# Issuing the second input load ahead of SyncE's arrival at the entry barrier

## Chip, cores, metric

One core of one Trainium2 chip; the other cores of the chip run nothing of this program. The metric is the device time of one execution in microseconds, the median of several runs.

## The reference

Each row of a 1024 x 4096 float32 matrix is divided by its length:

```python
def reference(x, axis, eps):            # axis = -1, eps = 1e-12
    norm = np.sqrt(np.sum(x ** 2, axis=axis, keepdims=True) + eps)
    return (x / norm).astype(np.float32)
```

16.78 MB are read and 16.78 MB written. There is little arithmetic.

## The kernel before

The rows are cut into two groups. A group is one tile of 128 partitions x 4 rows x 4096 elements, 64 KB a partition, moved by one load and one store of 8.39 MB each. Both loads are issued by SyncE before any work; the stores are issued by SyncE as well, each when its group is done. ScalarE squares and sums three rows of a group and VectorE one; VectorE does most of the scaling.

The program begins with a barrier at which all engines meet. The kernel before already moves its first load to the front of it, when the program is finalized:

```python
def first_load_to_front(nc, load):
    def move(program):
        blocks = program.main_func.blocks
        entry = blocks[0].instructions
        ...                                   # body: the block that holds the load; at: its place
        assert not body[at].sync_info.on_wait
        before = next(n for n, i in enumerate(entry)
                      if i.engine == SP and isinstance(i, InstDrain))
        entry.insert(before, body.pop(at))    # ahead of SyncE's drain, its arrival at the barrier
    nc.at_finalize(move)

...
    for i in range(n_tiles):                  # n_tiles = 2
        g = RowGroups(nc, io, stats, scratch, D, R, eps_t)
        load = nc.sync.dma_start(out=g.flat(), in_=x_t[i])
        if i == 0:
            first_load_to_front(nc, load.ins)
        groups.append(g)

    for i, g in enumerate(groups):
        ...                                   # squares, norms, scalings of one group
        store = nc.sync.dma_start(out=out_t[i], in_=g.flat())
```

## Time and profile before

| | before |
|---|---|
| time, median of the first 3 runs | 81.92 us (81.86 to 81.96) |
| profiled execution: time, span | 82.04 us, 80.20 us |
| first load: issued, landed | 0.00, 22.06 us |
| second load: issued, landed | 0.79, 41.37 us |
| first store: issued, landed | 38.99, 60.72 us |
| second store: issued, landed | 56.76, 80.03 us |

"Issued" is the start of the issue on SyncE; "landed" is the last of the sixteen increments of the transfer's semaphore, one from each DMA engine. All are counted from the span's start. The four landings lie 19.31 to 19.35 us apart, whatever the four issue times are. The lines of the profile that carry this are in the prediction below.

### The profile page before, as it was taken

The numbers are of one execution on the slowest core, as the hardware profiler recorded it, in microseconds if no ns is written. First come the engines' busy times: TensorE is split into PE (matmuls) and PEld (weight loads), VectorE is DVE, ScalarE is ACT, GpSimd is POOL, SyncE is SP. The second block draws the span as 40 slices with busy tenths as digits, with TensorE's granted clock in tenths as the row PEclk, the third lists the DMA queues.
The fourth block names the chain that finished last, engine by engine and source line by source line (L and its number), as shares of the span: only waits on it lengthen the run. The fifth ranks groups of instructions, "written<-read, shape, count | busy, mean of one in ns | idle before, by whom it ended". The sixth has DMA issues, their size and how long they took to land.

```text
span 80.2 us, 93 instructions
## 1 busy us (share of the span) xinstructions
DVE 26.7 (33%) x21; ACT 29.7 (37%) x23; POOL 0.2 (0%) x4
## 2 busy tenths in 40 slices
DVE  0000000000099599960039995999200000000000
ACT  6000000000099999989439999950000000000000
POOL 0000000000000000000000000000000000000000
DMA  9099996699996699996699990999991999992990
GB/s 490 33 523 523 523 490 294 261 523 523 523 490 261 294 523 523 523 490 261 294 523 523 523 490 33 523 523 523 523 458 65 523 523 523 523 425 98 523 523 0
DMA packets 576, 33.55 MB, mean 418 GB/s; under 512 B 64, under 2 KB 64, under 8 KB 64
## 3 DMA queue, kind: packets, MB, share of 16 engines
q1 hardware_dynamic: 576, 33.55, 97.4%
HBM read 16.78 MB, written 16.78 MB: 418 GB/s over the span
## 4 chain that ended last, share of the span: by engine, by line
DMA 51%; ACT 10%; DVE 9%; issue 0%
DMA xt<-in_x_dram 51%; ACT sq_act L33 9%; DVE xt L64 9%; ACT rstd L53 1%; DVE rstd L59 0%
## 5 line engine op out<-in xcount | busy, mean ns | idle before, releaser
L33 ACT ACTIVATE sq_act<-xt 128x4096 f32<-128x4096 f32 x6 | 21.7, 3609 | 22.4 <-DMA xt<-in_x_dram 22.4
L42 DVE SCALAR_TENSOR_TENSOR sq_dve<-xt 128x4096 f32<-128x4096 f32 x2 | 8.9, 4426 | 26.4 <-DMA xt<-in_x_dram 26.4
L64 DVE TENSOR_SCALAR xt<-xt,rstd 128x4096 f32<-128x4096 f32 x7 | 16.5, 2353 | 0.2
L72 ACT ACTIVATE xt<-xt,rstd 128x3584 f32<-128x3584 f32 x1 | 3.3, 3283 | 0.2 <-DVE rstd L59 0.2
L53 ACT ACTIVATE rstd<-ssq,eps_t 128x1 f32<-128x1 f32 x8 | 2.1, 290 | 0.1
L59 DVE RECIPROCAL rstd<-rstd 128x1 f32<-128x1 f32 x8 | 1.3, 160 | 2.5 <-ACT rstd L53 2.5
L33 ACT ACT_TABLE_LOAD x1 | 1.3, 1283 | 0.8 <-PEq L258 0.8
L53 ACT ACT_TABLE_LOAD x1 | 1.3, 1283 | 0.0
L33 ACT ACTIVATION_READ_ACCUMULATOR sq_act<-xt 128x1 f32 x6 | 1.1, 187 | 0.0
L78 DVE TENSOR_SCALAR xt<-xt,rstd 128x512 f32<-128x512 f32 x1 | 0.5, 487 | 0.0
L211 DVE MEMSET eps_t<- 128x1 f32 x1 | 0.1, 59 | 0.9 <-PEq L258 0.9
L42 DVE DVE_READ_ACCUMULATOR sq_dve<-xt 128x1 f32 x2 | 0.2, 83 | 0.0
L258 POOL MEMSET const-uint8-127<- 128x1 uint8 x1 | 0.1, 103 | 0.0
L258 POOL MEMSET const-bfloat16-1.0<- 128x1 bf16 x1 | 0.1, 102 | 0.0
L258 POOL MEMSET const-float32-0.0<- 128x1 f32 x1 | 0.1, 99 | 0.2 <-issue 0.2
L258 POOL MEMSET const-float32-1.0<- 128x1 f32 x1 | 0.1, 99 | 0.0
## 6 DMA issues: line engine op xcount, KB each, us to landing
xt<-in_x_dram SPq DMA_DIRECT2D x2, 31.3
out_dram<-xt SPq DMA_DIRECT2D x2, 22.5
```

Of the source, the lines that this page charges most:

```text
L33: self.nc.scalar.activation(out=sq_a, in_=self.x[:, r], func=ACT_F.Square, accum_out=self.ssq[:, r : r + 1],)
L42: self.nc.vector.scalar_tensor_tensor(out=sq_v, in0=self.x[:, r], scalar=1.0, in1=self.x[:, r], op0=ALU.mult, op1=ALU.mult, accum_out=self ...
L53: self.nc.scalar.activation(out=self.rstd[:, r : r + n], in_=self.ssq[:, r : r + n], func=ACT_F.Sqrt, bias=self.eps_t,)
L59: self.nc.vector.reciprocal(out=self.rstd[:, r : r + n], in_=self.rstd[:, r : r + n])
L64: self.nc.vector.tensor_scalar_mul(out=self.x[:, r], in0=self.x[:, r], scalar1=self.rstd[:, r : r + 1])
L72: self.nc.scalar.activation(out=self.x[:, r, :cut], in_=self.x[:, r, :cut], func=ACT_F.Copy, scale=rstd,)
L78: self.nc.vector.tensor_scalar_mul(out=self.x[:, r, cut:], in0=self.x[:, r, cut:], scalar1=rstd)
L211: nc.vector.memset(eps_t, eps)
L258: nc = _bacc.Bacc("TRN2", target_bir_lowering=False, num_devices=1)
```

## The change

The second load is moved ahead of the barrier too. The intent is to have both transfers with the DMA engines as soon as possible, at the price of SyncE's arriving later.

```diff
-def first_load_to_front(nc, load):
+def to_front(nc, load):
...
         load = nc.sync.dma_start(out=g.flat(), in_=x_t[i])
-        if i == 0:
-            first_load_to_front(nc, load.ins)
+        to_front(nc, load.ins)
         groups.append(g)
```

## The prediction

> **What bounds the kernel now.** I read the page of the kernel before first, then the chain of work that ended last, then the start in order of time, then who the DMA queue waited for, and last the records of single packets.
>
> The page:
>
> ```profile
> span 80.2 us, 93 instructions
> DVE 26.7 (33%) x21; ACT 29.7 (37%) x23; POOL 0.2 (0%) x4
> ...
> GB/s 490 33 523 523 523 490 294 261 523 523 523 490 261 294 523 523 523 490 261 294 523 523 523 490 33 523 523 523 523 458 65 523 523 523 523 425 98 523 523 0
> ...
> q1 hardware_dynamic: 576, 33.55, 97.4%
> ```
>
> VectorE and ScalarE are idle nearly two thirds of the time; the one DMA queue is at work 97.4% of the span. The rows of 40 slices mislead here: slices of 33 and 65 GB/s look like holes, the second of them right behind the start, just where this change works. A slice is 80.2 / 40 = 2.0 us, a packet of this kernel (65,536 bytes in the packet records) takes 2.42 us, the sixteen engines run nearly in step, and a packet is counted where it starts. So a slice catches sixteen starts (16 x 65,536 B / 2.0 us = 523 GB/s) or few; longer stretches show 442 GB/s (4 to 42 us) and 437 (42 to 78 us). The holes are none.
>
> The chain that ended last names the loads for half the span, and then stops at the last scaling at 56.7 us, because it follows instructions and the last store is none:
>
> ```profile
> 0.73 0.07 issue
> 0.79 40.58 DMA xt<-in_x_dram
> 41.37 0.02 issue
> ```
>
> "0.79 40.58" looks as if the second load, which the change moves, took 40.58 us from its issue, so that an earlier issue would end it earlier. The packet records say otherwise. Following each engine's packets end to start, the slowest engine starts its first at 1.97, ends it at 4.80, ends its share of the first load at 21.72, of the second at 41.06, of the first store at 60.38 and of the last at 79.70 us. Those are steps of 19.32 to 19.34 us, eight packets of 2.416 us each, with no gap at any of the three borders. The second load waits for the first one's packets, not for its own issue.
>
> The start, and the queue's own waits:
>
> ```profile
> 0.00 0.38 SPq L219 DMA_DIRECT2D xt<-in_x_dram  x1
> ...
> 0.79 1.28 ACT L33 ACT_TABLE_LOAD   x1 [0.79 <-PEq L258]
> 0.79 0.33 SPq L219 DMA_DIRECT2D xt<-in_x_dram  x1
> 0.86 0.06 DVE L211 MEMSET eps_t<- 128x1 f32 x1 [0.86 <-PEq L258]
> ```
>
> ```profile
> SPq L240 <- DVE xt L64: 15.3, 1, 15.3
> SPq L272 <- DMA out_dram<-xt: 3.2, 1, 3.2
> SPq L240 <- ACT xt L72: 2.8, 1, 2.8
> SPq L240 <- DMA xt<-in_x_dram: 2.0, 1, 2.0
> SPq L258 <- PEq L258: 0.2, 1, 0.2
> ```
>
> SyncE issues the first load at 0, arrives at the barrier, is released at 0.71, issues the second at 0.79. The barrier costs it 0.2 us of waiting (last row). The other engines start at 0.79 to 0.86 and then wait until 22.08 us for the first load.
>
> So the end is the slowest engine's sum: first packet at 1.97, that packet 2.83 (longer than the rest), 31 more at 2.416 = 74.90, together 79.70; 0.33 until its semaphore (80.03), 0.17 for the final release (80.20). The profiled execution was timed at 82.04, so 1.84 us lie outside the span.
>
> **What the Trainium skill says.** Three places.
> "DMA: Bandwidth & Descriptors", section "Where 436 GB/s comes from": 16 ports x 32 B x 850 MHz = 435.2 GB/s as the ceiling of the fabric. The trace agrees: 16 x 65,536 B / 2.416 us = 434 GB/s. Nothing about when a transfer is issued can speed that up.
> The same page, section "Queues, rings and completion order": on each DMA engine, descriptors of one issuing engine's queue are consumed in ring order. The trace agrees: both loads are on q1 and the second follows the first without a gap.
> "Perfetto Trace Analysis", section "Per-instruction lifecycle: what the profiler-reported window actually captures": the window of a hardware-generated DMA covers lock, descriptor generation and the sequencer's semaphore push; the data movement is outside it. The trace agrees: windows of 0.38 and 0.33 us against landings at 22.06 and 41.37 us.
>
> **The change part by part.** No instruction is added or removed. Comparing the order on each engine, the only difference is on SyncE: load, barrier, load becomes load, load, barrier. The first load stays first at time 0, so the start of the span does not move.
>
> 1. The second load's issue. Before, SyncE's drain began 0.05 us after the first issue's end at 0.38; now the second issue should take that place, from about 0.40 to 0.75 us (0.33 to 0.38 us long). It comes 0.79 - 0.40 = 0.39 us earlier. What that buys: the first load's first packet began 1.02 us after its issue began, so by the same delay the second load was ready from 0.79 + 1.02 = 1.81 us on, while the earliest engine is done with the first load at 20.94 us. It sat ready for 19.1 us; it now sits for 19.5. Gain on the path: 0.
>
> 2. The barrier. SyncE arrives later by one issue and its step, 0.35 to 0.4 us. Before, GpSimd saw all arrivals at 0.59 and released at 0.67; now about 0.98 and 1.06. The table load goes from 0.79 to about 1.17 and ends near 2.45 instead of 2.07; the memset from 0.86 to 1.24. Both wait for 22.08 us afterwards, so the slack is 19.6 us. Loss on the path: 0.
>
> 3. The first store. It is issued at 38.99, 16.93 us after the first load's landing at 22.06; with 1.02 us from issue to packet it is ready at about 40.0. The fastest engine runs out of load packets at 40.27, the slowest at 41.06. The slack is only 0.27 us on the fastest engine, the tightest place here, but 1.05 us on the one that sets the end. Both sides of it hang on the same packets, so a shift of the whole start leaves it as it is; only a wider spread of the engines could eat it, and first on engines that have 0.3 us to spare at the end. Effect: 0.
>
> 4. The first packets. This is what I cannot work out. Eleven engines start between 1.02 and 1.20 us, three at 1.48 to 1.51, and two at 1.97 and 2.12; the one at 1.97 later ends last. In the kernel before, the second load's issue lies at 0.79 to 1.13, so its descriptors, by the delay of 0.63 us from the first issue's end to the first packet, come up at about 1.4 to 1.8 us, just when the late five start. If that is why they are late, an earlier second issue moves it by 0.39 us. Every later packet runs at a fixed pace, so a shift of the slowest engine's first packet goes into the end one to one, until another engine is the last: the next ones end at 79.51, 79.48 and 79.43.
>
> Sum: 0 + 0 + 0, and a term of the start between about -0.3 and +0.35.
>
> **The rivals.**
> First, the late starters are due to the second issue and get earlier. For: the times above match. Against: the first packet is slow in all engines (2.42 to 3.36 us), so a cold start explains lateness as well. If all five move by 0.39, the end is set by an engine that ends at 79.43: gain 79.70 - 79.43 = 0.27, time 81.65. I give it a third.
> Second, the second load's descriptor work now falls at 0.4 to 0.75 us, before any packet of the first has started, and holds the first load's packets up. For: both pass through one issuer. Against: the first issue has ended by then, and its descriptors lie ahead in the ring. If the whole start slips by one issue, 0.35 us is lost: 82.27. One in ten.
> Third, the chain read at face value: the second load ends 0.39 us earlier, and so does everything: 81.53. Against it stands the gapless border at 21.72 us. One in twenty.
> Fourth, the later barrier delays the compute enough to open a gap before the first store. It would need the 19.6 us of slack to be false; under one in a hundred.
>
> **Range and chances.** The bulk of the weight, just over half, is on nothing at all, 81.92. A third at -0.27 and a twentieth at -0.39 against a tenth at +0.35 give about -0.07: 81.85 us. The three runs before spread over 0.10 us; another chip might add 0.1 to 0.2 (my guess). Range 81.55 to 82.20. A step of 2% is 1.64 us. To win it, the start would have to shrink from 79.70 - 32 x 2.416 = 2.39 us to 0.75, less than the 1.02 us from the unmoved first issue to the first packet; to lose it, a whole delay of four issues would have to reach the DMA engines. So 0.975 for within 2%.
>
> **What would show it.** In the profile after: two issues back to back at 0 and about 0.4 us; the table load near 1.17; first load's landing near 22.06 and the second's 19.3 us later, whatever its issue; the first store issued 16.9 us after the first landing; packet time unchanged at 2.42 us with no gap; the last landing 58.0 us after the first (80.03 - 22.06). The whole difference in span must then be the difference of the slowest engine's first packet. If the late starters sit 0.39 us earlier, the first rival is right; if the first packet itself begins later than 1.02, the second. I am wrong in the mechanism if the distance between the two landings changes by more than 0.1 us, or a gap stands before the store's packets; and in the size if the time leaves the range.

## The result, and the profile after

The changed kernel took 81.88 us (median of 6 runs, 81.73 to 81.98), the kernel before 81.93 (6 runs, 81.73 to 81.96). The ratio is 0.9997 with a 95% interval of 0.9982 to 1.0011: no difference of even 0.2% is seen. (Ratios here and below are the mean time of one kernel's fast runs over that of the other's of the same rounds, so not quite the ratio of the medians quoted.)

The page of the changed kernel, its first line and the line of its DMA queue (packets, MB, share of 16 engines' span):

```profile
span 79.9 us, 93 instructions
...
q1 hardware_dynamic: 576, 33.55, 97.6%
```

The start in order of time (start, length in us), from 0.4 us on:

```profile
0.43 0.43 SPq L219 DMA_DIRECT2D xt<-in_x_dram  x1
1.26 1.28 ACT L33 ACT_TABLE_LOAD   x1 [1.26 <-PEq L257]
1.33 0.06 DVE L211 MEMSET eps_t<- 128x1 f32 x1 [1.33 <-PEq L257]
```

The second issue stands at 0.43 instead of 0.79 us, so 0.36 earlier; ScalarE and VectorE start 0.47 us later (1.26 and 1.33 for 0.79 and 0.86). Both parts of the change took place. Neither shows further on. The stretch around 40 us, first of the kernel before:

```profile
38.99 0.35 SPq L240 DMA_DIRECT2D out_dram<-xt  x1
41.40 3.62 ACT L33 ACTIVATE sq_act<-xt 128x4096 f32<-128x4096 f32 x1 [2.43 <-DMA xt<-in_x_dram]
```

and of the changed one:

```profile
38.71 0.35 SPq L239 DMA_DIRECT2D out_dram<-xt  x1
...
41.15 3.62 ACT L33 ACTIVATE sq_act<-xt 128x4096 f32<-128x4096 f32 x1 [2.46 <-DMA xt<-in_x_dram]
```

The first store and the second group's start are both 0.25 to 0.28 us earlier, and so was the first landing already, at 21.79 for 22.06. The whole of it comes from the first packets: the engine that ends last finished its first packet at 4.54 us here and at 4.80 there, 0.26 us, and the spans differ by 0.27. That isn't the change's gain: the timings of the two kernels cover the same range, and the profiled execution of the kernel before was simply one of its longer ones (82.04 us).

The chain that ended last shows again why it is not to be taken at its word. In the changed kernel it has this line for the second load (start, length):

```profile
0.43 40.69 DMA xt<-in_x_dram
```

It had 0.79 and 40.58 before. The load was issued 0.36 us earlier and took 0.11 us longer from there to its end; the rest is the 0.25 of the start.

### The profile page after: what moved, and what is told of

Read it like the earlier page. It is cut to its first block, busy times and chain, and to the rows that moved or that the text cites. A ratio compares the mean times of both kernels' runs of the same rounds, so it can differ in the third digit from the quotient of the medians.

```text
span 79.9 us, 93 instructions
## 1 busy us (share of the span) xinstructions
DVE 26.7 (33%) x21; ACT 29.7 (37%) x23; POOL 0.2 (0%) x4
## 4 chain that ended last, share of the span: by engine, by line
DMA 51%; ACT 10%; DVE 9%; SPq 0%; issue 0%
DMA xt<-in_x_dram 51%; ACT sq_act L33 9%; DVE xt L64 9%; ACT rstd L53 1%; SPq L219 0%; DVE rstd L59 0%
```

## The experiments

My theory: a DMA queued behind another on the same queue gains nothing from an earlier issue, as long as it is there before the engines run out of packets. The rivals: the earlier issue is worth its 0.36 us and the later barrier takes that back; or the two issues next to each other change how the first load starts. "Before" in each paragraph is the kernel before, timed on the same chip in the same rounds.

### Second load issued at 14.7 us

```diff
+        if i == 1:
+            for r in range(R):
+                nc.gpsimd.memset(g.x[:, r], 0.0)
         load = nc.sync.dma_start(out=g.flat(), in_=x_t[i])
```

(The kernel before, so the second load is not moved; the memsets write into its tile, and it has to wait for them.)

> The kernel before, with four GpSimd memsets of 128x4096 into the second load's tile ahead of it, so that the second load is issued late (my guess is between 8 and 20 us instead of 0.79). Theory (the second load only has to be queued before the engines run out of the first one's packets at 20.9 us): no change, 81.7 to 82.1, ratio to the kernel before within 0.3%, the two landings still 19.3 us apart, as long as issue + 1.0 us stays below 20.9; past that it lengthens one to one. Rival (the earlier issue is worth its 0.39 us, and something else gave it back): slower by the delay, 8 us or more. Rival on the start (the second issue causes the late starters): the engines that start their first packet at 1.5 to 2.1 us all start before 1.25 us here; if a cold start causes them, five late ones stay.

81.86 us against 81.91, ratio 0.9995 (0.9982 to 1.0009), correct. Its order of time:

```profile
0.79 13.85 POOL L221 MEMSET xt<- 128x4096 f32 x4 [0.35 <-POOLq L261]
...
14.66 0.33 SPq L222 DMA_DIRECT2D xt<-in_x_dram  x1
```

```profile
38.69 0.35 SPq L243 DMA_DIRECT2D out_dram<-xt  x1
41.19 3.62 ACT L33 ACTIVATE sq_act<-xt 128x4096 f32<-128x4096 f32 x1 [2.52 <-DMA xt<-in_x_dram]
```

The second load was issued 13.87 us later than in the kernel before and landed at 41.10 us, 19.32 after the first. Issue time within the slack is worth nothing, in either direction; the rival of two effects that cancel is gone, because here the delay is 38 times as long and the barrier is where it was.

### Second load issued at 25.0 us

Seven memsets instead of four, in the same place.

> As second_late, with seven memsets instead of four: at 3.46 us each the second load is issued near 25.0 us, after the engines ran out of the first one's packets (20.9 to 21.7 us). Theory (a slack, then one to one): a load issued at 0 landed at 21.8 to 22.1, so this one lands near 46.9; the kernel before needs 38.66 us from that landing to the last one, so the span is 85.7 and the time 87.5 us. The first store is then issued near 38.9, some 7 us before the second load ends; if a store that is queued long ahead of the loads' end stalls the engines, as the cut first load seems to show (1.1 us there), it is 88.6 us. Rival (the load's issue time never matters): 81.9.

88.64 us against 81.82, ratio 1.083 (1.081 to 1.084), correct.

```profile
25.00 0.33 SPq L222 DMA_DIRECT2D xt<-in_x_dram  x1
...
48.02 3.62 ACT L33 ACTIVATE sq_act<-xt 128x4096 f32<-128x4096 f32 x1 [9.44 <-DMA xt<-in_x_dram]
```

The first packets of the second load start at 25.96 us, 0.96 after its issue, on engines that have stood still. So the slack is real, and it ends between the two issue times tried, 14.66 and 25.00 us. The engines ran out of the first load's packets at 20.88 to 21.36 us here; less the 0.96 that is 19.9 to 20.4, and the loss taken one to one (6.8 us less 1.1 for the stall told below) gives 19.3; both are estimates. The load landed at 47.94, and 22.9 us after its issue is 1.1 us more than a first load takes; its last packets took 3.18 to 3.88 us. That excess was expected because of the run with the first load cut into four, told below; this one was made after it.

### Neither load moved

```diff
-        if i == 0:
-            first_load_to_front(nc, load.ins)
```

> Neither load moved: both come after the barrier. Theory (only the first issue starts the clock of the DMA engines, every packet after it follows without a gap): the first load is issued about 0.70 us later than in the kernel before, so 82.5 to 82.7 us, slower by 0.7 to 0.9%. Rival (the barrier's place does not matter for the first load either, its delay is hidden by the cold start): within 0.2%, 81.9.

82.63 us against 81.91, ratio 1.0088 (1.0074 to 1.0101), correct.

```profile
0.73 0.85 SPq L219 DMA_DIRECT2D xt<-in_x_dram  x2
...
22.61 3.62 ACT L33 ACTIVATE sq_act<-xt 128x4096 f32<-128x4096 f32 x1 [20.60 <-DMA xt<-in_x_dram]
```

With the first load at 0.73 us, the time is 0.72 us longer. The first load's place ahead of the barrier is worth about its 0.73 us (0.6 to 0.8 by the interval); the second load's, nothing.

### Second load on another engine's queue

```diff
-        load = nc.sync.dma_start(out=g.flat(), in_=x_t[i])
+        load = (nc.sync if i == 0 else nc.scalar).dma_start(out=g.flat(), in_=x_t[i])
```

> The second load is issued by ScalarE after the barrier, at about the same 0.8 us, on that engine's own queue; the first stays ahead on SyncE. Theory (the second load is harmless early because one queue keeps it behind the first): two queues share the DMA engines packet by packet, the first load lands near 38 to 41 us instead of 22, the first store is issued near 55 to 58 us, and the DMA engines stand still from 41 to then: 95 to 100 us. Rival (issue order alone decides, whatever the queue): 81.9 us with landings at 22 and 41.

101.28 us against 81.91, ratio 1.236 (1.234 to 1.238), correct. The page's row of GB/s and its queues (packets, MB, share of 16 engines' span), and the order of time:

```profile
GB/s 422 422 422 422 422 422 422 422 422 422 422 422 422 422 422 422 0 0 0 0 0 0 0 0 422 422 422 422 422 606 580 501 422 422 422 422 422 422 422 0
...
q1 hardware_dynamic: 432, 25.17, 59.2%
q10 hardware_dynamic: 144, 8.39, 19.5%
```

```profile
0.78 0.37 ACTq L219 DMA_DIRECT2D xt<-in_x_dram  x1
...
38.91 3.62 ACT L33 ACTIVATE sq_act<-xt 128x4096 f32<-128x4096 f32 x1 [36.45 <-DMA xt<-in_x_dram]
...
59.12 10.96 SPq L240 DMA_DIRECT2D out_dram<-xt  x2
```

The issue is again at 0.78 us, as in the kernel before, and only the queue is another. Now the first load lands at 38.89 us instead of 22.06 and the second at 41.28, the engines have nothing to store, and eight slices of 2.5 us are a true hole of zeros. The Trainium skill, "DMA: Bandwidth & Descriptors", section "Queues, rings and completion order", says that a DMA engine goes round-robin, packet by packet, between the queue rows that have work; the two landings, 2.4 us apart, agree, and so do the packet records: after two packets of the first load, the engines take one of q10 and one of q1 in turn until the first load is done. So early issue is harmless here because of the one queue, which keeps the second load behind the first. (The time is above my 95 to 100 us: the first store was issued at 59.12, later than I had put it, for VectorE took the second group's square, 4.4 us, before the first group's scalings.)

### First load cut into four, all five loads ahead of the barrier

```diff
-        load = nc.sync.dma_start(out=g.flat(), in_=x_t[i])
-        to_front(nc, load.ins)
+        step = D if i == 0 else R * D
+        for at in range(0, R * D, step):
+            part = slice(at, at + step)
+            load = nc.sync.dma_start(out=g.flat()[:, part], in_=x_t[i][:, part])
+            to_front(nc, load.ins)
```

> The changed kernel with the first load cut into four of one row each (128x4096, 16 KB a packet), all five loads ahead of the barrier. SyncE then arrives near 2.3 us and the other engines start near 2.7 us. Theory (a late barrier costs nothing, an issue of 0.4 us feeds 4.8 us of packets): 81.4 to 82.2 us, first load complete near 22 us; smaller first packets may take up to 0.3 us off the start. Rival (the engines' late start or the extra issues reach the end): 83.5 us or more, 1.7 us longer.

83.12 us against 81.91, ratio 1.0143 (1.0128 to 1.0157), correct. My number was missed by 1 us, and the rival's, which blamed the barrier, was near it. The order of time:

```profile
2.81 1.28 ACT L33 ACT_TABLE_LOAD   x1 [2.81 <-PEq L260]
...
29.42 0.35 SPq L242 DMA_DIRECT2D out_dram<-xt  x1
42.44 3.62 ACT L33 ACTIVATE sq_act<-xt 128x4096 f32<-128x4096 f32 x1 [15.68 <-DMA xt<-in_x_dram]
```

The engines start 2.0 us later than in the kernel before, and yet the first load is complete at 21.97 us, as ever. The loss comes later: the second load lands 20.44 us after the first instead of 19.33. The packet records show where. All sixteen engines take 3.13 to 3.70 us for their last load packet, which starts at 38.0 to 38.4 us, instead of 2.42; no other packet after the start is that slow. What is different at that moment is the first store. Work on the first group began as soon as its first row had landed, so the store was issued at 29.42 and lay in the queue for 9 us before the last load packets. Two explanations were left: A, a store queued long ahead stalls the engines at the change from loads to stores; B, it is the number of transfers or the packet size. The next runs are for that.

### A store that is early without any cut

The changed kernel: the arithmetic on the first group is left out (`if i > 0:` before it), and its store is issued as soon as its load has landed.

> Wrong on purpose: the changed kernel without any arithmetic on the first group, whose store is issued as soon as its load has landed, near 21.9 us, 19 us before the second load ends. Nothing else is changed. A: a store queued long ahead of the loads' end stalls the engines at the change from loads to stores: 83.0 us, all sixteen engines with one packet of 3.1 to 3.7 us near 38 to 41 us. B: the stall of the cut first load came from its number of transfers or its packet size: 81.9 us, no packet over 2.5 us after the start.

83.03 us against 81.82, ratio 1.0144 (1.0128 to 1.0160), results wrong.

```profile
21.81 36.82 SPq L240 DMA_DIRECT2D out_dram<-xt  x2
42.31 3.62 ACT L33 ACTIVATE sq_act<-xt 128x4096 f32<-128x4096 f32 x1 [39.77 <-DMA xt<-in_x_dram]
```

(Two issues are merged in the first line; the first is at 21.81.) Whole loads, packets of 64 KB, four transfers, and the same stall: 3.21 to 3.79 us for the last load packet on all engines. B falls. It shows in the row of GB/s from 37 to 45 us, in slices of 0.2 us, where a packet counts in the slice in which it starts:

```profile
GB/s 0 0 0 0 1638 1966 1638 0 0 0 0 0 0 0 0 0 0 0 0 0 0 328 2622 983 1311 0 0 0 0 0 0 0 0 0 2621 1311 983 328 0 0
```

From the last load packets (the first group of numbers) to the first packets of the store (the second) it is 17 or 18 slices, about 3.5 us; from those to the next, 12 or 13, so about 2.4.

### The store held back by steps

The kernel with the cut load, and n multiplications of one row by 1.0 between the last scaling and the first store, to move its issue and nothing else:

```diff
+        if i == 0:
+            for _ in range(n):
+                nc.vector.tensor_scalar_mul(out=g.x[:, R - 1], in0=g.x[:, R - 1], scalar1=1.0)
         store = nc.sync.dma_start(out=out_t[i], in_=g.flat())
```

n = 2:

> The changed kernel with the first load in four (rows_ahead, 83.12 us, first store issued at 29.4) and two multiplications by 1.0 of one row (2.35 us each) between its last scaling and the first store, which is then issued near 34.1 us. A (a store queued long ahead stalls): still 83.1 if 6 us ahead is as bad as 11, with the stall in the last load packet. B (transfers or packet size): 83.1 as well, so this run tells little alone and stands beside the next one.

n = 4:

> As rows_held2 with four multiplications, so that the first store is issued near 38.8 us, as in the kernels before and after (39.0 and 38.7). A (a store queued long ahead stalls): 81.8 to 82.0, no packet over 2.5 us after the start. B (number of transfers or packet size): 83.1, the stall stays.

n = 3, and n = 3 with half a row more:

> Three multiplications: the first store is issued near 36.3 us, so by the 1.0 us from issue to packet it is ready near 37.3, before any engine starts its last load packet (37.9 to 38.4 us). If what counts is that the store is queued when the last load packet starts, the stall of 1.1 us is there: 83.0 us. If what counts is a longer lead (the 4 us of rows_held2), it is gone: 81.9.

> Three and a half multiplications: first store issued near 37.5 us and ready near 38.5, just after the last load packets have started. Queued before the start counts: 81.9 us, the last load packets at 2.42 us. If it is enough that the store arrives within the last packet, part of the stall: 82.2 to 83.0.

n = 5:

> Five multiplications: first store issued near 40.9 us and ready near 41.9, after the engines ran out of load packets (40.2 to 40.9 us). Theory (a late store opens a gap): the first store's packets start 1.0 to 1.7 us late, 82.9 to 83.4 us, a gap of at least 1 us on every engine and no packet of 3 us in the loads. If the room on the late side is larger than I worked out: 81.9.

All five were correct. The kernel with the cut load and the changed kernel stand beside them; packet times are from the packet records.

| run | first store issued, us | last load packet, us | second load landed, us | time, us | ratio to before (95%) |
|---|---|---|---|---|---|
| no hold | 29.42 | 3.13 to 3.70 | 42.41 | 83.12 | 1.0143 (1.0128 to 1.0157) |
| n = 2 | 33.96 | 3.10 to 3.85 | 42.43 | 83.07 | 1.0143 (1.0126 to 1.0161) |
| n = 3 | 36.35 | 3.49 to 3.83 | 42.60 | 83.13 | 1.0156 (1.0138 to 1.0173) |
| n = 3.5 | 37.62 | 2.42 to 3.02 | 41.53 | 82.29 | 1.0056 (1.0039 to 1.0073) |
| n = 4 | 38.59 | 2.42 to 2.55 | 41.29 | 81.89 | 0.9998 (0.9979 to 1.0016) |
| the change | 38.71 | 2.42 to 2.43 | 41.12 | 81.88 | 0.9997 (0.9982 to 1.0011) |
| n = 5 | 41.00 | 2.42 | 41.26 | 83.24 | 1.0172 (1.0155 to 1.0188) |

The store's issue and the start of the second group, which tells the second load's landing, in order of time with n = 4:

```profile
38.59 0.35 SPq L247 DMA_DIRECT2D out_dram<-xt  x1
41.31 3.62 ACT L33 ACTIVATE sq_act<-xt 128x4096 f32<-128x4096 f32 x1 [14.69 <-DMA xt<-in_x_dram]
```

its row of GB/s from 37 to 45 us, with steps of 12 slices throughout,

```profile
GB/s 0 0 0 0 0 1966 3277 0 0 0 0 0 0 0 0 0 0 1311 3605 328 0 0 0 0 0 0 0 0 0 983 3932 328 0 0 0 0 0 0 0 0
```

and the order of time with n = 5:

```profile
41.00 0.35 SPq L247 DMA_DIRECT2D out_dram<-xt  x1
41.28 3.62 ACT L33 ACTIVATE sq_act<-xt 128x4096 f32<-128x4096 f32 x1 [14.58 <-DMA xt<-in_x_dram]
```

With n = 4 the cut load costs nothing: neither three more transfers nor a barrier 2.0 us later is seen in the time. Explanation A holds. With n = 5 the loads end undisturbed at 40.36 to 40.80 us, but the store's packets begin only at 41.85 to 42.00, at the earliest 0.85 us after its issue; every engine stands still for 1.05 to 1.64 us, and that gap is the loss. So the early side of the window for the first store's issue lies between 37.62 and 38.59 us, and its late side below 41.00, by estimate near 39.5 (40.36 less 0.85). The kernel before (38.99) and the changed one (38.71) both sit in that window as far as the time goes, the kernel before so late that some of its engines already waited (point 3 below). My rule for the early side, that the store must not be ready when the last load packet starts, was not quite right: with n = 3.5 it was ready after those starts (37.62 + 0.85 = 38.47, an estimate, against 37.94 to 38.34) and cost 0.4 us all the same. How the time falls off between 37.6 and 38.6 us, and what in the DMA engines stalls, stays open.

## Why the prediction was right

The time, 81.88 us, lies 0.03 from the 81.85 predicted. That closeness is luck: the mechanism alone gave 81.92, the rivals' weights made 81.85 of it, and none of them is borne out. What was right is that nothing is gained and nothing lost.

1. The second load's issue. Predicted: 0.39 us earlier, gain 0. Seen: 0.36 us earlier, no gain; and the slack behind it (19 us by the sum) was shown from both sides, by the issue at 14.7 us that cost nothing and the one at 25.0 that cost 6.8 (1.1 of it the stall of the early store).

2. The barrier. Predicted: 0.35 to 0.4 us later, loss 0. Seen: 0.47, because the second issue took 0.43 us at this place instead of the 0.33 it took before. The loss is 0, up to the 2.0 us of the run with n = 4.

3. The first store. Predicted: 16.9 us after the first landing. Seen: 38.71 - 21.79 = 16.92. That nothing would come of it was right, but the working was wrong on the late side and silent on the early one. On the late side I had the store ready near 40.0 us, 1.02 after its issue, with 0.27 us to spare on the fastest engine. In the packet records of the kernel before no packet of the store starts before 40.48, 1.49 us after its issue, when engines had been running out of load packets since 40.27; added up, the sixteen engines waited 1.1 us there (one trace). The slowest, which ran out at 41.05, did not wait, so the end did not move. In the changed kernel, with the store at 38.71, the waits add up to 0.04 us, and its time is the same. The store also has an early side: next to the 38.99 us of the kernel before, a store at 37.62 cost 0.4 us and one at 36.35 or earlier 1.2 to 1.3. The change moves the store with the first landing, and that landing did not move.

4. The first packets. Predicted: the difference in span is that of the slowest engine's first packet. Seen: 0.27 against 0.26. The last landing followed the first by 79.76 - 21.79 = 57.97 us (58.0 predicted). The first packet of all began 1.01 us after the first issue, as before, so the sign named for the second rival is not there.

The first rival, to which I gave a third, is not borne out: after the change five engines still start their first packet after 1.3 us, the last at 2.04, where an earlier start by 0.39 was asked for. Without a second load near, one such engine was left (issue at 14.7) or two (25.0), which would speak for it; but the wrong-on-purpose kernel has the start of the changed one and showed two, so the number varies by itself, with one trace of each (four with neither load moved, five on the other queue). What makes an engine late is not settled. It matters little: engines that start late have a shorter first packet, and with whole loads the slowest first packet ended 4.45 to 4.80 us after the first issue in all seven traces, with whatever number of late engines. The second rival (0.35 us lost at the start) and the third (0.39 gained by the chain at face value) are excluded by an interval of -0.2 to +0.1%, and so is the 0.27 us of the first (0.33%).

## What to carry to other kernels

Where transfers follow each other in one queue without a gap, the issue time of any but the first is slack; find it by laying the landings side by side (equal distances) and not from the chain, which counts a transfer from its issue. Equal distances of the last landings speak for the slowest engine alone; whether others wait, the packet records show. Only the first issue of a dry queue is worth moving. Before moving a later one, look at what it could run into: on another queue it would have shared the engines with the first load and cost 24%, and a store that was queued too early behind loads cost 1.4 to 1.6% when it was issued about 1.8 us or more before the last load packets started.

## What the Trainium skill lacked or had wrong

- "DMA: Bandwidth & Descriptors" has nothing on a store queued early behind loads of the same queue. Here it made the last load packet of all sixteen engines take 3.1 to 3.9 us instead of 2.42 and cost 1.1 to 1.3 us in five runs, while a load queued behind a load cost nothing. The advice in its section "Rules for kernel authors" to issue a DMA early and wait for it late needs this exception.
- The same page, section "Where 436 GB/s comes from", says that for transfers between HBM and SBUF the HBM side of about 358 GB/s binds. The sentence doesn't say that this is for two cores at once, as the note under the page's own table of bandwidths (425 GB/s, one core) does. With one core at work the packets of loads and stores ran at 16 x 65,536 B / 2.416 us = 434 GB/s here, close to the fabric's ceiling that the section gives.
- No page has that the first packets of a load are slow on engines that stood still, or that the engines don't begin together: at the start of the program the first 64 KB packet of an engine took up to 3.5 us for 2.42, and the engines began 1.0 to 2.1 us after the start of the issue; the load issued at 25.0 us had first packets of 2.66 to 3.29. The store did not show it: after 19 us of standing still (second load on another engine's queue) its first packets took 2.45 to 2.47.
